# A hybrid RWKV-7 and Gated DeltaNet block: the bonus behind the pair products, dense products in groups of four, two output tiles interleaved

## The chip, the cores and the metric

The kernel runs on one core of one Trainium2 chip. The metric is the device time of one execution in microseconds; the times of the kernel before are the median, the lowest and the highest of three runs.

## What is computed

One layer of a streaming encoder over 512 positions of width 1024, all in float32. Cut to what matters here:

```python
u = rms_norm(x, norm1_g)
p = u @ w_in                                   # rwkv part, qkv, z, a, b, two gates
y_a = rwkv7_mix(...) @ rwkv_proj               # 8 heads of 64
y_b = gated_deltanet_mix(...) @ gdn_proj       # 4 heads of 128
mixed = sigmoid(gate_a) * y_a + sigmoid(gate_b) * y_b
x = x + mixed @ w_out
h = causal_depthwise_conv(rms_norm(x, norm2_g) @ ffn_up, ffn_conv_w)
h_gate, h_up = split(h)
x = x + (silu(h_gate) * h_up) @ ffn_down
return rms_norm(x, final_g)

# inside rwkv7_mix, behind the scan over positions:
y = group_norm_heads(y, ln_w, ln_b)
y = y + sum(r_h * k_h * r_k, axis=-1) * v_h    # the bonus
```

## The kernel before, in words

**Layout.** Activations lie transposed, 128 channels on the partitions and 512 positions in the free dimension, so a width of 1024 is eight K-tiles. Every dense product is made of float32 weights and activations that are each split into a high and a low half: `halves_of` (L156, L158) makes the halves `hi` (on ACT) and `lo` (on POOL or DVE in turn) of 512 columns of a weight tile `raw`, and `split` (L201 to L205) those of an activation, `uh` and `ul`.

**Dense products.** `mm3` (L173 to L185) adds lo x uh, hi x uh and hi x ul in one PSUM bank: for each half of a weight tile (four K-tiles) eight matmuls of L180 and L181 in turn, then four of L183, so 12 a half and 24 a tile. They number 2496 in mm3: 1056 for w_in, 192 for the two branch projections, 192 for w_out and 1056 for ffn_up. Banks come from three groups, D (2 banks, dense tiles), A (3) and B (3, the second stream).

**Stages by time.** First tiles to 50 us; the mixing from 50 to 430 us, in which the dense tiles of w_in run between the work of the heads; the projections of the two branches (`project(0)`, `project(1)`), 430 to 476 us; w_out, 476 to 520; ffn_up to 765; ffn_down to the end.

**The mixing.** The string `ORDER` lists its parts: R0 to R3 prepare one RWKV head pair each (`rwkv_prep`), I0 and I1, or i0 and i1, invert triangular matrices (L563 to L569 on DVE, L591 and L598 on PE), z0 to z3 hold the output gates of the DeltaNet heads, g0 to g13 dense tiles of the two merge gates, c0 and c1 are the chains over chunks of the RWKV heads (L661 to L674: matmuls of 64 rows and columns, `Z` and `SUV` evacuated between them by DVE and ACT), G0 to G3 and C0, C1 the same for the DeltaNet heads (C1's last matmul is L928). What an engine executes next is settled by a list scheduler from the program order and the priorities (`tc.high_priority`, `stream2`), not by the text alone.

**One preparation** (`rwkv_prep`) makes, on DVE, the scaled keys (L508, L510, L513, tile `BK`, one buffer for each half of the chunks), then the bonus: r * r_k * K on DVE (L515), a matmul with a block of ones on PE (L517), the product with v on DVE into `yf` (L518). Behind it, for each half h, the pairwise products of four chunks on PE into two banks (`pe`, L527, and `po`, L528) and transposes into a third (`pt`, L530), the masked copies on DVE (L534, four) and a copy on ACT (L537); at the end one scaling on DVE (L538). All these banks are of group A.

**The output projection** (`merge`, L966 to L980) takes the eight tiles of w_out one after the other. Its operand `uh`, `ul` comes from project(1): per tile DVE adds (L946, L948), ACT makes uh (L204) and DVE ul (L205).

Of the kernel before, what the change touches and what calls it, by code (L numbers as in the profile page):

```python
# [13 lines left out]
ALU = mybir.AluOpType  # L14
# [3 lines left out]
D = 1024  # L18
# [6 lines left out]
BANKS = {"D": 2, "A": 3, "B": 3}  # L25
ORDER = "R0 g0 R1 g1 g2 g3 a i0 G0 G1 z1 c0 z0 g4 g5 R2 I0 R3 C0 g6 i1 c1 g7 g8 G2 G3 g9 z3 g10 z2 g11 I1 g12 C1 g13"
RAWG = 1
UN = (range(0), range(2), range(2, 8))
NWARM = 13
OUTG = ((0, 2), (2, 4), (4, 6), (6, 8))  # L30
# [64 lines left out]
class Body:  # L95
# [74 lines left out]
        return parts  # L170


    def mm3(self, ps, parts, act, first=True, last=True):  # L173
        nc = self.nc
        k0 = 0
        for i, (wh, wl, n) in enumerate(parts):
            w = [slice(k * 128, k * 128 + 128) for k in range(n)]
            x = [act(k0 + k) for k in range(n)]
            for k in range(n):
                nc.tensor.matmul(ps, wl[:, w[k]], x[k][0], start=(first and i == 0 and k == 0), stop=False)  # L180
                nc.tensor.matmul(ps, wh[:, w[k]], x[k][0], start=False, stop=False)  # L181
            for k in range(n):
                nc.tensor.matmul(ps, wh[:, w[k]], x[k][1], start=False,  # L183
                                 stop=(last and i == len(parts) - 1 and k == n - 1))
            k0 += n  # L185

    def dense_in(self, m, act=None, tag="D", parts=None):
# [257 lines left out]
    def rwkv_prep(self, hp, first=None):  # L445
        nc = self.nc
        Rt, K, r = first or (self.rp.tile([128, 9, T], F32, tag="R", name=self.nm("R")), self.t("P"), self.t("P"))
# [4 lines left out]
        v = Rt[:, 8, :]  # L452
        if first is None:
# [5 lines left out]
        ps = self.bank()  # L459
# [8 lines left out]
                                     op0=ALU.mult, op1=ALU.add)  # L468
# [10 lines left out]
        ps = self.bank()  # L479
# [11 lines left out]
        for tl, s in ((ase, slice(0, 64)), (aso, slice(64, 128))):  # L491
            nc.vector.scalar_tensor_tensor(out=tl[s, :, 0, :], in0=kv[s], scalar=self.nkk[s, hp:hp + 1], in1=ep[s, :, 0:64],
                                           op0=ALU.mult, op1=ALU.mult)
            self.on("e").tensor_tensor(out=tl[s, :, 1, :], in0=rv[s], in1=ep[s, :, 1:65], op=ALU.mult)

        ps = self.bank()
# [8 lines left out]
        q = lambda x, s, h: x[s, h * 256:h * 256 + 256].rearrange("p (c t) -> p c t", c=4)  # L505
# [6 lines left out]
            for s, sk in ((slice(0, 64), 1), (slice(64, 128), 0)):  # L512
                self.on("c").tensor_tensor(out=bkh[h][s, :, sk, :], in0=q(K, s, h), in1=q(em, s, h), op=ALU.mult)  # L513

        nc.vector.scalar_tensor_tensor(out=r, in0=r, scalar=self.vec("r_k", hp), in1=K, op0=ALU.mult, op1=ALU.mult)  # L515
        ps = self.bank()
        nc.tensor.matmul(ps, self.con("bones"), r, start=True, stop=True)  # L517
        nc.vector.tensor_tensor(out=self.yf[:, hp, :], in0=ps, in1=v, op=ALU.mult)  # L518

        rwm = self.con("rwm")  # L520
        for h in range(2):
            pe, po, pt = self.bank(), self.bank(), self.bank()
# [8 lines left out]
            w = slice(4 * h, 4 * h + 4)  # L531
            lo, hi = slice(0, 64), slice(64, 128)
            for ps, s, tl in ((pe, lo, ntb), (pe, hi, ase), (po, hi, ntb), (po, lo, aso)):
# [3 lines left out]
            nc.scalar.activation(bkt[:, w, :], pt.rearrange("p (c t) -> p c t", c=4), AF.Copy)  # L537
        self.on("o").tensor_tensor(out=ntb[:, :, 0, :], in0=ntb[:, :, 0, :],  # L538
                                in1=rs2.unsqueeze(2).broadcast_to([128, 8, 64]), op=ALU.mult)
        return dict(ase=ase, aso=aso, ntb=ntb, bkt=bkt, v=v)  # L540

    def inv(self, x):
# [409 lines left out]
    def merge(self):  # L952
# [12 lines left out]
        self.u2p = self.pool("u2p", bufs=1, reuse_waits="tile")  # L965
        self.u2h = self.u2p.tile([128, KD, T], F32R, name="u2h")  # L966
        self.u2l = self.u2p.tile([128, KD, T], F32R, name="u2l")
        for m in range(KD):
            parts = self.unit(self.a["w_out"][m])
            ps = self.bank("D")  # L970
            self.mm3(ps, parts, lambda k: (mh[:, k, :], ml[:, k, :]))
            x = x1[:, m, :]
            g = self.vec("norm2", m)
            with tc.high_priority():
                nc.vector.tensor_tensor(out=x, in0=ps, in1=x, op=ALU.add)
                nc.scalar.activation(self.u2h[:, m, :], x, AF.Copy, scale=g)
                nc.vector.scalar_tensor_tensor(out=self.u2l[:, m, :], in0=x, scalar=g, in1=self.u2h[:, m, :].bitcast(F32),
                                               op0=ALU.mult, op1=ALU.subtract)
            self.sumsq(self.acc2, x, m == 0)
# [267 lines left out]
```

## Time and profile before

| | |
|---|---|
| time, median of 3 runs | 893.6 us (893.51 to 896.17) |
| the profiled execution: time | 897.17 us |
| the profiled execution: span from first to last instruction | 895.0 us |
| mean granted clock of TensorE | 0.992 |
| PE busy | 860.9 us, 96% |
| PE weight loads (beside the matmuls) | 677.9 us, 76% |
| DVE, ACT, POOL busy | 646.0, 473.2, 209.7 us |
| bytes moved | 84.25 MB, 94 GB/s |

PE is TensorE's matmuls, DVE is VectorE, ACT ScalarE, POOL GpSimd. The span is what the rows further down divide; the execution's own time has 2.2 us around it. A row of a timeline has the start, the duration, the engine, the line of the kernel, the tile written and the tiles read, and in brackets how long the engine sat idle before it and what ended that. Matmuls overlap: the pace is the distance of their starts, not their duration.

### The profile page before, as it was taken

Reading aid. Unit: us, or ns where it says so; the run is one execution under the profiler, and the core shown is the slowest. Engines: PE = TensorE matmul, PEld = TensorE weight load, DVE = VectorE, ACT = ScalarE, POOL = GpSimd, SP = SyncE. Lnnn points to the kernel's source line nnn. Section 1 sums busy time; section 2 is a strip of 40 time slices with the busy share of each in tenths; the row PEclk is TensorE's granted clock in tenths of the full one; section 3 lists DMA queues with packets and bytes.
Section 4 is the critical chain, followed back from the end, with each engine's and each line's share of the span. In section 5 each row is a group of like instructions: output and inputs, shape, how many; then the busy total and the mean of one; then the engine's idle time right before and its main releaser. Section 6 shows DMA issues by size and latency. Waiting matters only on the chain.

```text
span 895.0 us, 13509 instructions
## 1 busy us (share of the span) xinstructions
PE 860.9 (96%) x5046; PEld 677.9 (76%) x5046; DVE 646.0 (72%) x1247; ACT 473.2 (53%) x909; POOL 209.7 (23%) x189
## 2 busy tenths in 40 slices
PE   7989999999999999999999999999999999999996
PEld 4867677666767777667787878888888888898895
DVE  6898797874888986855476448988866666573565
ACT  7745457667443777673543455455444444444433
POOL 2231123111121221111212222222222222352431
PEclk9999999999999999999999999999999999999998
DMA  7321222121212221125352323323333332332333
GB/s 263 112 91 59 71 71 72 48 73 48 72 59 71 71 72 37 60 89 206 94 174 85 94 95 94 95 94 95 94 100 101 101 100 90 99 102 86 110 86 133
DMA packets 29746, 84.25 MB, mean 94 GB/s; under 512 B 3312, under 2 KB 5488, under 8 KB 29680
## 3 DMA queue, kind: packets, MB, share of 16 engines
q1 hardware_dynamic: 29680, 83.39, 29.3%
q8 instruction: 40, 0.66, 0.3%
q14 instruction: 26, 0.21, 0.1%
HBM read 77.61 MB, written 5.77 MB: 93 GB/s over the span
## 4 chain that ended last, share of the span: by engine, by line
PE 70%; DVE 19%; ACT 4%; issue 4%; DMA 1%; POOL 1%; SPq 0%; DVEq 0%; POOLq 0%; ACTq 0%
PE D L183 15%; PE D L180 15%; PE D L181 15%; PE D L1077 5%; PE A L1077 4%; PE B L1077 3%; DVE lo L158 2%; DVE R L534 1%; DVE P L769 1%; DMA raw<-w_in 1%; DVE invN L563 1%; DVE BK L513 1%; DVE invY L565 1%; DVE BK L508 1%; DVE R L948 1%
## 5 line engine op out<-in xcount | busy, mean ns | idle before, releaser
L158 POOL TENSOR_TENSOR lo<-raw,hi 128x512 fp32r<-128x512 f32 x124 | 170.3, 1373 | 614.4 <-ACT hi L156 590.6
L156 ACT ACTIVATE hi<-raw 128x512 fp32r<-128x512 f32 x248 | 152.9, 620 | 195.7 <-PE D L183 95.2
L180 PE MATMUL D<-uh,lo 128*128 128x512 f32 x384 | 158.3, 413 | 3.5 <-ACT uh L204 1.9
L181 PE MATMUL D<-uh,hi 128*128 128x512 f32 x384 | 157.6, 410 | 0.0
L180 PE MATMUL D<-u2h,lo 128*128 128x512 f32 x352 | 137.9, 392 | 0.0
L181 PE MATMUL D<-u2h,hi 128*128 128x512 f32 x352 | 137.8, 392 | 0.0
L183 PE MATMUL D<-ul,hi 128*128 128x512 f32 x384 | 117.8, 411 | 0.4 <-DVE ul L202 0.4
L158 DVE TENSOR_TENSOR lo<-raw,hi 128x512 fp32r<-128x512 f32 x124 | 87.7, 707 | 34.9 <-ACT hi L156 34.5
L183 PE MATMUL D<-u2l,hi 128*128 128x512 f32 x352 | 95.1, 392 | 0.0
L180 PEld LDWEIGHTS D<-uh,lo 128*128 128x128 f32 x384 | 72.7, 189 | 21.8 <-ACT uh L204 2.4
L181 PEld LDWEIGHTS D<-uh,hi 128*128 128x128 f32 x384 | 72.6, 189 | 16.0 <-issue 1.0
L994 DVE SCALAR_TENSOR_TENSOR P<-T,vecs,P 128x511 f32<-128x511 f32 x88 | 78.3, 890 | 8.4 <-ACT P L992 4.1
L183 PEld LDWEIGHTS D<-ul,hi 128*128 128x128 f32 x384 | 70.4, 189 | 17.1 <-issue 1.2
L181 PEld LDWEIGHTS D<-u2h,hi 128*128 128x128 f32 x352 | 66.1, 188 | 14.9 <-issue 0.2
L180 PEld LDWEIGHTS D<-u2h,lo 128*128 128x128 f32 x352 | 66.1, 188 | 14.7 <-issue 0.2
L183 PEld LDWEIGHTS D<-u2l,hi 128*128 128x128 f32 x352 | 66.1, 188 | 14.1
L991 DVE TENSOR_TENSOR T<-D,acc 128x512 f32<-128x512 f32 x44 | 30.3, 688 | 34.5 <-PE D L183 30.6
L992 ACT ACTIVATE P<-T,vecs 128x512 f32<-128x512 f32 x44 | 31.7, 721 | 12.1 <-DVE T L991 10.0
L563 DVE TENSOR_TENSOR invN<-invA,invY 128x60 f32<-128x60 f32 (+24 forms) x124 | 33.2, 268 | 2.6
L565 DVE TENSOR_TENSOR invY<-invY,invN 128x60 f32<-128x60 f32 (+24 forms) x124 | 33.0, 266 | 2.9
L769 DVE SCALAR_TENSOR_TENSOR P<-D,vecs,P 128x511 f32<-128x511 f32 (+2 forms) x36 | 26.6, 740 | 1.5 <-ACT P L767 1.5
L1183 ACT ACTIVATE P<-P 128x512 f32<-128x512 f32 x22 | 13.7, 624 | 18.7 <-DVE P L994 18.7
(437 smaller groups left out, 1566.1 us busy)
## 6 DMA issues: line engine op xcount, KB each, us to landing
raw<-w_in SPq DMA_DIRECT2D x44, 512.0 KB, 3.5
raw<-ffn_up SPq DMA_DIRECT2D x44, 512.0 KB, 3.6
raw<-ffn_down SPq DMA_DIRECT2D x9, 512.0 KB, 3.5
raw<-w_out SPq DMA_DIRECT2D x8, 512.0 KB, 3.6
raw<-ffn_down SPq DMA_DIRECT2D x16, 256.0 KB, 2.9
spill<-T SPq DMA_DIRECT2D x14, 256.0 KB, 2.0
R<-spill SPq DMA_DIRECT2D x14, 256.0 KB, 5.9
raw<-ffn_down SPq DMA_DIRECT2D x9, 384.0 KB, 3.1
```

Source lines behind the costliest of these rows:

```text
L156: nc.scalar.activation(hi[:, 0:w], raw[:, o:o + w], AF.Copy)
L158: self.on(str(self.halves % 4)).tensor_tensor(out=lo[:, 0:w], in0=raw[:, o:o + w], in1=hi[:, 0:w].bitcast(F32), op=ALU.subtract)
L180: nc.tensor.matmul(ps, wl[:, w[k]], x[k][0], start=(first and i == 0 and k == 0), stop=False)
L181: nc.tensor.matmul(ps, wh[:, w[k]], x[k][0], start=False, stop=False)
L183: nc.tensor.matmul(ps, wh[:, w[k]], x[k][1], start=False, stop=(last and i == len(parts) - 1 and k == n - 1))
L563: nc.vector.tensor_tensor(out=w, in0=rows[:, t, 0:t].unsqueeze(2).broadcast_to([128, t, n]), in1=Ym[:, t, c:G].unsqueeze(1).broadcast_to([ ...
L565: nc.vector.tensor_tensor(out=Ym[:, 0:t, c:G], in0=Ym[:, 0:t, c:G], in1=w, op=ALU.add)
L769: nc.vector.scalar_tensor_tensor(out=cv[:, sh:], in0=ps[:, 0:T - sh], scalar=w(3 - sh), in1=cv[:, sh:], op0=ALU.mult, op1=ALU.add)
L991: nc.vector.tensor_tensor(out=h, in0=ps, in1=self.acc2, op=ALU.mult)
L992: nc.scalar.activation(cv, h, AF.Copy, scale=w(2))
L994: nc.vector.scalar_tensor_tensor(out=cv[:, sh:], in0=h[:, 0:T - sh], scalar=w(2 - sh), in1=cv[:, sh:], op0=ALU.mult, op1=ALU.add)
L1077: nc.tensor.matmul(out, w, x, start=bank not in started, stop=stop)
```

## The change

`rwkv_prep` issues the bonus (multiply, matmul, product with v) at its end, behind both halves of the pairwise products. `mm3` gives every matmul but the first of each four a high priority, so that the scheduler keeps the four together; the order of the 12 matmuls is as before. `merge` takes w_out's tiles 0 and 1 half by half: tile 0 with K-tiles 0 to 3, tile 1 with 0 to 3, tile 0 with 4 to 7, tile 1 with 4 to 7. From line 28 on the lines move by 2 and more: L180, L181 and L183 become L185, the bonus L538, L540 and L541, the products L524, L525 and L527, the masked copies L531, the chain steps L663 and on.

```diff
--- before.py
+++ after.py
@@ -25,6 +25,8 @@
 BANKS = {"D": 2, "A": 3, "B": 3}
 ORDER = "R0 g0 R1 g1 g2 g3 a i0 G0 G1 z1 c0 z0 g4 g5 R2 I0 R3 C0 g6 i1 c1 g7 g8 G2 G3 g9 z3 g10 z2 g11 I1 g12 C1 g13"
 RAWG = 1
+
+BLK = 4
 UN = (range(0), range(2), range(2, 8))
 NWARM = 13
 OUTG = ((0, 2), (2, 4), (4, 6), (6, 8))
@@ -170,18 +172,18 @@
         return parts
 
 
+
     def mm3(self, ps, parts, act, first=True, last=True):
         nc = self.nc
         k0 = 0
         for i, (wh, wl, n) in enumerate(parts):
             w = [slice(k * 128, k * 128 + 128) for k in range(n)]
             x = [act(k0 + k) for k in range(n)]
-            for k in range(n):
-                nc.tensor.matmul(ps, wl[:, w[k]], x[k][0], start=(first and i == 0 and k == 0), stop=False)
-                nc.tensor.matmul(ps, wh[:, w[k]], x[k][0], start=False, stop=False)
-            for k in range(n):
-                nc.tensor.matmul(ps, wh[:, w[k]], x[k][1], start=False,
-                                 stop=(last and i == len(parts) - 1 and k == n - 1))
+            seq = [(t, 0, k) for k in range(n) for t in (wl, wh)] + [(wh, 1, k) for k in range(n)]
+            for q, (t, p, k) in enumerate(seq):
+                with self.tc.high_priority(offset=100000) if q % BLK else nullcontext():
+                    nc.tensor.matmul(ps, t[:, w[k]], x[k][p], start=(first and i == 0 and q == 0),
+                                     stop=(last and i == len(parts) - 1 and q == len(seq) - 1))
             k0 += n
 
     def dense_in(self, m, act=None, tag="D", parts=None):
@@ -512,11 +514,6 @@
             for s, sk in ((slice(0, 64), 1), (slice(64, 128), 0)):
                 self.on("c").tensor_tensor(out=bkh[h][s, :, sk, :], in0=q(K, s, h), in1=q(em, s, h), op=ALU.mult)
 
-        nc.vector.scalar_tensor_tensor(out=r, in0=r, scalar=self.vec("r_k", hp), in1=K, op0=ALU.mult, op1=ALU.mult)
-        ps = self.bank()
-        nc.tensor.matmul(ps, self.con("bones"), r, start=True, stop=True)
-        nc.vector.tensor_tensor(out=self.yf[:, hp, :], in0=ps, in1=v, op=ALU.mult)
-
         rwm = self.con("rwm")
         for h in range(2):
             pe, po, pt = self.bank(), self.bank(), self.bank()
@@ -537,6 +534,11 @@
             nc.scalar.activation(bkt[:, w, :], pt.rearrange("p (c t) -> p c t", c=4), AF.Copy)
         self.on("o").tensor_tensor(out=ntb[:, :, 0, :], in0=ntb[:, :, 0, :],
                                 in1=rs2.unsqueeze(2).broadcast_to([128, 8, 64]), op=ALU.mult)
+
+        nc.vector.scalar_tensor_tensor(out=r, in0=r, scalar=self.vec("r_k", hp), in1=K, op0=ALU.mult, op1=ALU.mult)
+        ps = self.bank()
+        nc.tensor.matmul(ps, self.con("bones"), r, start=True, stop=True)
+        nc.vector.tensor_tensor(out=self.yf[:, hp, :], in0=ps, in1=v, op=ALU.mult)
         return dict(ase=ase, aso=aso, ntb=ntb, bkt=bkt, v=v)
 
     def inv(self, x):
@@ -965,10 +967,20 @@
         self.u2p = self.pool("u2p", bufs=1, reuse_waits="tile")
         self.u2h = self.u2p.tile([128, KD, T], F32R, name="u2h")
         self.u2l = self.u2p.tile([128, KD, T], F32R, name="u2l")
+
+
+        mixed = lambda k: (mh[:, k, :], ml[:, k, :])
+        two = [(self.unit(self.a["w_out"][m]), self.bank("D")) for m in range(2)]
+        for q in range(2):
+            for parts, ps in two:
+                self.mm3(ps, parts[q:q + 1], lambda k: mixed(4 * q + k), first=q == 0, last=q == 1)
         for m in range(KD):
-            parts = self.unit(self.a["w_out"][m])
-            ps = self.bank("D")
-            self.mm3(ps, parts, lambda k: (mh[:, k, :], ml[:, k, :]))
+            if m < 2:
+                ps = two[m][1]
+            else:
+                parts = self.unit(self.a["w_out"][m])
+                ps = self.bank("D")
+                self.mm3(ps, parts, mixed)
             x = x1[:, m, :]
             g = self.vec("norm2", m)
             with tc.high_priority():
```

Where the scheduler puts the matmuls is seen from the order of PE's instructions. The first place is the preparation of the first head pair; `P_287` is r * r_k * K, `BK_511` and `BK_512` the two halves' keys, D tiles are dense products. Before:

```order
L183 MATMUL D_654<-ul,hi_650 128x512 x4
L517 MATMUL A_523<-P_287,cons 128x512
L527 MATMUL A_526<-R_285,BK_511 128x128
L528 MATMUL A_527<-R_285,BK_511 128x128
...
L530 MATMUL A_528<-cons,BK_511 128x128 x4
...
L527 MATMUL A_546<-R_285,BK_512 128x128
L528 MATMUL A_547<-R_285,BK_512 128x128
...
L530 MATMUL A_548<-cons,BK_512 128x128 x4
```

With the change:

```order
L524 MATMUL A_522<-R_285,BK_511 128x128
L525 MATMUL A_523<-R_285,BK_511 128x128
...
L527 MATMUL A_524<-cons,BK_511 128x128 x4
L185 MATMUL D_654<-ul,hi_650 128x512 x4
L524 MATMUL A_542<-R_285,BK_512 128x128 x3
L525 MATMUL A_543<-R_285,BK_512 128x128 x3
...
L527 MATMUL A_544<-cons,BK_512 128x128 x4
L185 MATMUL D_785<-ul,hi_777 128x512 x4
L540 MATMUL A_564<-P_287,cons 128x512
```

The bonus matmul stood ahead of both halves' products and now stands behind them; the second half's products come behind four dense matmuls instead of seven.

The second place is the third step of the second RWKV chain, c1 (`B_2974` its bank). Before:

```order
L180 MATMUL D_3768<-uh,lo_3761 128x512
L181 MATMUL D_3768<-uh,hi_3760 128x512
L661 MATMUL B_2974<-SUV_2961,R_2016 64x64
L180 MATMUL D_3768<-uh,lo_3761 128x512
L662 MATMUL B_2974<-SUV_2962,R_2016 64x64
L181 MATMUL D_3768<-uh,hi_3760 128x512
L661 MATMUL B_2974<-SUV_2961,R_2387 64x64
L662 MATMUL B_2974<-SUV_2962,R_2387 64x64
L180 MATMUL D_3768<-uh,lo_3761 128x512
```

With the change:

```order
L185 MATMUL D_3729<-uh,hi_3725 128x512
L663 MATMUL B_2974<-SUV_2961,R_2016 64x64
L664 MATMUL B_2974<-SUV_2962,R_2016 64x64
L663 MATMUL B_2974<-SUV_2961,R_2387 64x64
L664 MATMUL B_2974<-SUV_2962,R_2387 64x64
L185 MATMUL D_3729<-ul,hi_3725 128x512 x4
L669 MATMUL B_2974<-Z_2979,R_2016 64x64 x2
```

The eight matmuls of the step (each row here is two) were cut by single dense ones and now stand together; over the whole program the runs that hold such matmuls go from 83 to 68, and the runs of dense matmuls from 149 to 135.

The third place is the begin of w_out on PE; `D_4720` is its tile 0, `D_4759` before and `D_4731` in the change its tile 1. Before:

```order
L183 MATMUL D_4720<-ul,hi_4712 128x512 x4
L180 MATMUL D_4720<-uh,lo_4717 128x512
...
L183 MATMUL D_4720<-ul,hi_4716 128x512 x4
L180 MATMUL D_4759<-uh,lo_4752 128x512
...
L183 MATMUL D_4759<-ul,hi_4751 128x512 x4
```

With the change:

```order
L185 MATMUL D_4720<-ul,hi_4712 128x512 x4
L185 MATMUL D_4731<-uh,lo_4724 128x512
...
L185 MATMUL D_4731<-ul,hi_4723 128x512 x4
L185 MATMUL D_4720<-uh,lo_4717 128x512
...
L185 MATMUL D_4720<-ul,hi_4716 128x512 x4
```

Tile 0's second half now stands 12 matmuls later.

## Rows read from the trace of the kernel before

**Rows 1.** The page, busy time by engine, and the clock in 40 slices.

```profile
PE 860.9 (96%) x5046; PEld 677.9 (76%) x5046; DVE 646.0 (72%) x1247; ACT 473.2 (53%) x909; POOL 209.7 (23%) x189
...
PEclk9999999999999999999999999999999999999998
```

**Rows 2.** Waits of PE: engine, bank, line, releaser: us, times, longest.

```profile
PE A L517 <- DVE P L515: 5.2, 4, 2.0
PE D L180 <- ACT uh L204: 1.9, 1, 1.9
...
PE B L598 <- ACT invY L594: 0.8, 1, 0.8
```

**Rows 3.** Windows: length, busy time (and instructions) by engine, granted clock, DMA.

```profile
69.00:72.50 3.50, 3.50 (x22) 2.88 (x21) 3.49 (x7) 0.51 (x1) 0.00 (x0) 0.51 0.27 70
...
80.00:120.00 40.00, 36.68 (x188) 27.26 (x187) 33.59 (x80) 20.91 (x46) 5.42 (x6) 1.00 0.20 73
...
482.00:485.50 3.50, 3.50 (x9) 2.72 (x10) 1.31 (x2) 1.05 (x2) 1.27 (x1) 0.52 0.41 140
485.50:489.00 3.50, 3.50 (x17) 2.80 (x16) 1.46 (x3) 1.89 (x4) 0.22 (x1) 1.00 0.45 121
```

**Rows 4.** Timeline of PE at the begin of w_out: start us, duration us.

```profile
475.67 0.40 PE L180 MATMUL D<-uh,lo 128*128 128x512 f32 x1
...
478.47 0.39 PE L180 MATMUL D<-uh,lo 128*128 128x512 f32 x1
...
481.96 0.69 PE L180 MATMUL D<-uh,lo 128*128 128x512 f32 x1 [1.94 <-ACT uh L204]
```

**Rows 5.** Timelines of ACT and of POOL in the same stretch.

```profile
478.09 0.63 ACT L204 ACTIVATE uh<-R 128x512 fp32r<-128x512 f32 x1 [1.96 <-DVE R L948]
...
481.28 0.63 ACT L204 ACTIVATE uh<-R 128x512 fp32r<-128x512 f32 x1 [2.04 <-DVE R L948]
...
476.21 1.30 POOL L158 TENSOR_TENSOR lo<-raw,hi 128x512 fp32r<-128x512 f32 x1 [5.00 <-ACT hi L156]
```

**Rows 6.** Timeline of PE, a chain step cut in three.

```profile
348.49 0.39 PE L181 MATMUL D<-uh,hi 128*128 128x512 f32 x1
...
349.49 0.33 PE L662 MATMUL B<-SUV,R 128*64 128x64 f32 x2
...
350.78 0.39 PE L181 MATMUL D<-uh,hi 128*128 128x512 f32 x1
```

**Rows 7.** Timeline of PE, a chain step in one run.

```profile
368.47 0.39 PE L181 MATMUL D<-uh,hi 128*128 128x512 f32 x1
368.79 0.27 PE L661 MATMUL B<-SUV,R 128*64 128x64 f32 x1
...
369.50 0.39 PE L181 MATMUL D<-uh,hi 128*128 128x512 f32 x1
```

**Rows 8.** Timeline of PE, the bonus of the first and second head pair.

```profile
67.75 1.12 PE L517 MATMUL A<-P,cons 128*128 128x512 f32 x2 [1.85 <-DVE P L515]
...
94.27 1.13 PE L517 MATMUL A<-P,cons 128*128 128x512 f32 x2 [2.00 <-DVE P L515]
```

**Rows 9.** Timeline of DVE in the first two preparations.

```profile
66.94 0.75 DVE L515 SCALAR_TENSOR_TENSOR P<-P,vecs,P 128x512 f32<-128x512 f32 x1
68.45 0.75 DVE L373 SCALAR_TENSOR_TENSOR P<-D,vecs,P 128x511 f32<-128x511 f32 x1 [0.76 <-ACT P L372]
...
70.97 2.69 DVE L534 TENSOR_TENSOR R<-A,cons 64x512 f32<-64x512 f32 x4
...
95.43 0.69 DVE L518 TENSOR_TENSOR yf<-A,R 128x512 f32<-128x512 f32 x1 [1.22 <-PE A L517]
```

**Rows 10.** Timelines of DVE and PE at the first inverse.

```profile
148.99 0.70 DVE L569 STREAM_TRANSPOSE invA<-invN 128x512 f32<-128x512 f32 x1
...
138.86 0.39 PE L180 MATMUL D<-uh,lo 128*128 128x512 f32 x1
...
149.75 1.20 PE L591 MATMUL B<-invA,R 32*32 32x32 f32 x64 [0.21 <-DVE invA L569]
```

## The prediction

> **What bounds the kernel.** I read the page's busy times first: PE is busy 860.9 us of a span of 895.0, DVE 646.0 [rows 1]. So the kernel is a stream of matmuls, and a change can win in three ways only: less idle time of PE, a higher granted clock, or fewer nanoseconds per matmul. The idle time is 895.0 - 860.9 = 34 us, the kernel's start and end included; in the view of PE's waits the largest cause is the bonus matmul of a head pair (5.2 us in 4 waits), and the next is the operand uh of the output projection (1.9 us, once) [rows 2]. The clock row of the page is 9 in every slice but the last [rows 1], yet a table of narrow windows finds two stretches at about half, 69.0 to 72.5 us and 482.0 to 485.5 us, and full clock right behind [rows 3]; each begins right behind one of those waits. What a half-clock stretch costs I read from its own row: 9 matmuls start in 482.0:485.5 and 17 in the next 3.5 us [rows 3], so some 6 to 8 dense matmuls of 0.23 us are lost, 1.5 us. The dense pace is 12 matmuls in 478.47 - 475.67 = 2.80 us, 0.233 us each [rows 4].
>
> **1. Output projection, two tiles interleaved.** Tile 0 starts its second half at 478.47 and at 481.96 has stood 1.94 us idle for the operand uh number 7 [rows 4], which ACT starts at 481.28 and takes 0.63 us for [rows 5]. In the change the 12 matmuls of tile 1's first half stand there: 12 x 0.233 = 2.8 us, until 481.27; uh number 7 is then wanted 6 matmuls later, at 482.7, 0.8 us after it is there. Tile 1's weights are in time: the low half that POOL makes starts at 476.21 and takes 1.30 us [rows 5], done 0.96 us before 478.47. The interleave puts nothing ahead of uh number 7 on ACT or DVE; that chain runs at one operand per 3.19 us (481.28 - 478.09 [rows 5]), slower than PE's 12 x 0.233 = 2.8 per tile, so it lags PE whenever PE arrives, and a gain upstream shifts both. Saved: 1.94 us of wait and the 1.5 us of half clock behind it, **-3.4 us**. Bounds: 0, if uh number 7 is late again by 2 us, to -3.4.
>
> **2. Dense products in groups of four.** A dense matmul stays full price wherever it stands; what the change saves is the price of a switch between dense matmuls and the 64-row matmuls of the recurrent chains. At 348.49 a chain step of eight such matmuls is cut in three by single dense ones: from 348.49 to 350.78, 2.29 us, four dense matmuls start (4 x 0.233 = 0.93), so the step costs 1.36 us [rows 6]. At 368.47 the same eight stand together: 1.03 us with two dense (0.47), so 0.56 us [rows 7]. Two more runs cost 0.80 us, 0.40 per run. By the order, the runs that hold such small matmuls fall from 83 to 68; seven of the fifteen are of exactly this chain step, the others of shorter kinds. 7 x 0.40 = 2.8 us and 15 x 0.40 = 6.0 us are the bounds; I take eleven, **-4.4 us**.
>
> Against this speaks a rule of the Trainium skill ("TensorE: Matmul & The Clock Gate", "What happens when you issue a matmul"): the queue of TensorE pulls the next weight load ahead of running matmuls when row groups do not conflict or the load goes to the background buffer, so that a neighbour of another shape need not cost anything. By it this part would be 0. The two rows above do not agree, 1.36 us against 0.56; it stays as a rival.
>
> **3. The bonus behind the pair products.** Today the bonus matmul waits for the multiply of DVE at 66.94 and PE sits idle 1.85 us and, in the second pair, 2.00 us [rows 8]; with the small waits of pairs 2 and 3 that is 5.2 us [rows 2], and one fall of the clock (1.5). All 6.7 us go. What is late next: PE now meets the pair products first, whose inputs DVE writes just ahead of the same multiply, and only three A banks exist. DVE's order is hardly changed: the multiply (0.75 us) still stands ahead of the mask multiplies of the first half (four in 2.69 us) [rows 9], and these empty the banks that the second half's products need. I walked the first pair by these durations: first half waits about 1.1 us for its inputs, second half about 1.0 for a bank, the bonus 0.5; second pair 1.2, 1.4, 0.4; the last two pairs, 0.3 and 0.8. That is again 6.7 us. What remains is that DVE loses waits of its own: 1.22 us before the bonus multiply of the second pair and 0.76 at 68.45 [rows 9]; it leaves the second pair some 2.7 us earlier. I book **-1.0 us**. Bounds: -6.7 (no new wait) to +10.1: if in all four pairs the second half waits for the whole 2.69 us and the clock falls (1.5), 16.8 - 6.7. The value lies with my walk since DVE works through these 2.69 us while PE has a group of four and four transposes to do.
>
> **4. What the new order moves elsewhere.** The order places the first matmuls of the triangular inverse behind dense number 360 instead of 400. PE passes number 360 at 138.86 today; the input comes from DVE at 148.99 + 0.70 = 149.7, and the wait at 149.75 is only 0.21 [rows 10]. DVE has some 8 instructions fewer ahead of it (five convolution steps, one low half and two more, 0.6 to 0.75 each: 5.9 us) and starts 2.7 us earlier, so it is done at 141.1. PE would wait 141.1 - 138.9 = 2.2 us, and longer by what it gained upstream, about 3 us. In exchange the waits now at 145 to 153 us go, 0.8 at the next inverse step [rows 2], 0.2 and 0.5 beside it: 1.5 us. Net **+1.5 us**; bounds -1.5 (DVE is there) to +6 (the 2.7 us don't come, and the clock falls). The second DeltaNet chain ends 33 to 44 dense matmuls later (some 8 to 10 us), with 72 dense matmuls (16.8 us) still ahead of its consumer and about 11 us of finishing work: cover 5.8 us, cost 0; if that cover is gone, the second projection waits. Loads, bytes and the feed-forward part (pure dense work) are untouched.
>
> **Sum:** -3.4 - 4.4 - 1.0 + 1.5 = -7.3 us. The profiled execution took 897.2 us, 3.6 above the median of 893.6; the forecast is 889.9 for it and **886.3 us** for the median.
>
> **Rivals.**
> A. *Switches cost nothing saved* (the rule above; or the switches saved are the cheap ones, such as groups of 128-row matmuls): part 2 is 0 and the sum -2.9, 890.7 us. For: half of the fifteen runs aren't of the priced kind. Against: rows 6 and 7. Chance 0.15.
> B. *The waits really vanish*: DVE's lead spreads, preparations cost 3 us less and the inverse is fed in time (-1.5): -3.4 - 4.4 - 4.0 - 1.5 = -13.3, 880.3 us. For: DVE has no wait left in the preparations. Against: DVE is busy nearly without a break there, each step 0.6 to 0.75 us behind the last [rows 9]. Chance 0.17.
> C. *Slower, by the A banks*: the products of each second half stand in PE's queue ahead of whole groups of dense matmuls, so PE can't fill the wait. With 2.69 us and a fall of the clock in every pair, -3.4 - 4.4 + 10.1 + 1.5 = +3.8, 897.4 us. It decides once the new idle time in the preparations passes 6.7 + 6.3 = 13 us, 3.2 us per pair where I have 1.7. For: only three banks; a wait of 1.85 us was enough for a fall at 69 us. Against: 2.00 us at 94.27 brought none, the clock of 80 to 120 us is 1.00 [rows 3]. Chance 0.10.
> D. *About no change*: half of C's waits, -2 to +2 us, 893 us. Chance 0.10. That the change doesn't do what it says is no case: in the order the groups and the interleave stand.
>
> **The numbers.** The forecast (-4.5 to -10.5 us) has 0.48. Measurements of this kernel tell 0.3%, 2.7 us, from no change. Faster by more: forecast 0.48, B 0.17, two thirds of A 0.10, and 0.02 of D: 0.77. Slower by more: most of C and a little of D, 0.09. The rest, 0.14, is within. The range 878.5 to 892.0 holds the forecast, A, two thirds of B and a third of D, 0.8 together; below it lies the rest of B, above it C.
>
> **What would show it.** Right: no wait at the output projection and full clock at 480 us; PE's waits view without the bonus line but with the pair products and the bonus matmul (released by DVE mask multiplies or ACT copies) at about 6 to 7 us in sum; chain steps of eight small matmuls in one run at 0.56 us; a wait of 2 to 4 us at the inverse near 138 us. Wrong: dense matmuls beside the chains as far apart as before (A); more than 13 us of waits in the preparations, or more than two half-clock stretches (C); the inverse without a wait (B).

## The result, and the profile after

The change takes the kernel from 894.2 to 889.7 us (medians of 4 runs each): ratio 0.995, 95% interval 0.9937 to 0.9962, 4.5 us faster. Timed again beside three variants it gave 889.2 us against 894.6, ratio 0.9944 (0.9927 to 0.9960). The forecast was 886.3 us, a gain of 7.3, with a range of 878.5 to 892.0: the sign and the range held, the gain was some 60% of the sum.

The profiled execution of the changed kernel took 889.34 us, 0.4 below its median; its span is 887.6. That of before took 897.17, 3.0 us above its median, so two profiles laid side by side show 7.8 us where the medians show 4.5. The first experiment shows where most of that comes from. The page of the change (busy time; granted clock in 40 slices):

```profile
PE 854.3 (96%) x5046; PEld 679.3 (77%) x5046; DVE 653.5 (74%) x1247; ACT 466.0 (53%) x905; POOL 210.3 (24%) x189
...
PEclk9999999999999999999999999999999999999998
```

PE is busy 6.6 us less than in [rows 1] with the same number of instructions, and still the engine that is never long idle. The largest waits of PE in the change (engine, bank, line, releaser: us, times, longest):

```profile
PE A L794 <- DVE G L775: 2.9, 2, 1.8
PE B L675 <- ACT SUV L672: 2.2, 6, 0.8
PE A L524 <- DVE BK L515: 1.5, 2, 1.3
PE D L303 <- ACT hi L158: 1.5, 1, 1.5
PE B L593 <- DVE invA L571: 1.4, 1, 1.4
PE D L185 <- DVE R L375: 1.4, 1, 1.4
```

Both large waits of [rows 2] are gone, and nothing of 5 us stands in their place; the waits are now many and short, at the DeltaNet preparation (L794), the chains (L675), the pair products (L524), the second inverse (L593). The windows that answer to [rows 3] (length, PE, PEld, DVE, ACT, POOL busy, granted clock, DMA):

```profile
69.00:72.50 3.50, 3.29 (x22) 2.48 (x21) 3.45 (x6) 1.60 (x3) 0.00 (x0) 1.00 0.00 0
478.00:481.50 3.50, 3.50 (x16) 2.81 (x15) 2.66 (x3) 2.10 (x5) 1.48 (x2) 1.00 0.49 147
480.00:520.00 40.00, 40.00 (x174) 32.18 (x173) 21.52 (x31) 19.08 (x31) 9.14 (x8) 1.00 0.30 96
```

Neither half-clock stretch (a granted clock of 0.5) is there in this execution. That is not so in every execution: of the ten timed runs of the change (four here, six further down) five have a mean granted clock of 0.997, like this one, and take 888.4 to 889.3 us; the other five have 0.994 or 0.995 and take 889.8 to 890.8, on the mean 1.4 us more.

For all kernels below I split the time from the first dense matmul of mm3 to the first of w_out into two accounts, summed from the timeline of PE: **waits** (what stands in brackets) and **matmul time** (from each start to the next, less the wait). Beside them stand the time at half clock in that stretch, and the sum of both accounts at the pair products and the bonus matmul of the four preparations.

| kernel | start to w_out | waits | matmul time | at half clock | pair products and bonus | ratio to before |
|---|---|---|---|---|---|---|
| before | 453.6 | 18.8 | 434.7 | 3.4 | 19.1 | 1 |
| e1 interleave alone | 451.9 | 17.1 | 434.8 | 3.4 | 16.4 | 0.9967 |
| e2 groups of four alone | 452.9 | 24.3 | 428.7 | 6.8 | 18.1 | 0.9996 |
| e3 bonus alone | 454.4 | 16.4 | 438.0 | 3.4 | 19.2 | 1.0019 |
| e4 interleave and groups | 451.4 | 24.2 | 427.1 | 3.4 | 16.6 | 0.9956 |
| the change | 450.3 | 20.2 | 430.0 | 0 | 18.0 | 0.9950 |
| e9 the change again | 450.1 | 20.2 | 429.9 | 0 | 18.0 | 0.9944 |

One trace is one execution, and two of them differ also where the program does not. Ahead of w_out, before and e1 issue the same instructions, and so do e2 and e4. Their traces differ by 1.5 to 1.7 us up to w_out and by up to 2.7 us in the column of the pair products, so differences of that size between two rows say nothing by themselves.

The rest of the gain lies in w_out: from its first dense matmul to the 48th behind it 14.95 us before and 11.18 in the change.

### The profile page after: what moved, and what is told of

Same layout as the page of the kernel before. It is cut to its first block, busy times and chain, and to the rows that moved or that the text cites. A ratio compares the mean times of both kernels' runs of the same rounds, so it can differ in the third digit from the quotient of the medians.

```text
span 887.6 us, 13504 instructions
## 1 busy us (share of the span) xinstructions
PE 854.3 (96%) x5046; PEld 679.3 (77%) x5046; DVE 653.5 (74%) x1247; ACT 466.0 (53%) x905; POOL 210.3 (24%) x189
## 4 chain that ended last, share of the span: by engine, by line
PE 68%; DVE 16%; ACT 6%; issue 3%; POOL 0%; DVEq 0%; ACTq 0%; POOLq 0%
PE D L185 43%; PE D L1089 5%; PE A L1089 4%; PE B L1089 3%; PE B L185 2%; DVE invN L565 2%; PE A L185 2%; DVE invY L567 2%; DVE P L771 1%; DVE lo L160 1%; DVE R L531 1%; DVE BK L510 1%; DVE BK L515 1%; ACT hi L158 1%; PE B L663 1%
## 5 line engine op out<-in xcount | busy, mean ns | idle before, releaser
L185 PE MATMUL D<-uh,lo 128*128 128x512 f32 x384 | 160.5, 418 | 2.7 <-DVE R L375 1.4
L185 PE MATMUL D<-uh,hi 128*128 128x512 f32 x384 | 151.4, 395 | 0.0
L185 PE MATMUL D<-u2h,lo 128*128 128x512 f32 x352 | 137.9, 392 | 0.0
L185 PE MATMUL D<-u2h,hi 128*128 128x512 f32 x352 | 137.8, 392 | 0.0
L185 PE MATMUL D<-ul,hi 128*128 128x512 f32 x384 | 109.1, 406 | 0.0
L185 PE MATMUL D<-u2l,hi 128*128 128x512 f32 x352 | 95.1, 392 | 0.0
L185 PEld LDWEIGHTS D<-uh,lo 128*128 128x128 f32 x384 | 72.2, 188 | 21.3 <-issue 3.1
L1006 DVE SCALAR_TENSOR_TENSOR P<-T,vecs,P 128x511 f32<-128x511 f32 x88 | 81.8, 929 | 6.9 <-ACT P L1004 2.6
L185 PEld LDWEIGHTS D<-uh,hi 128*128 128x128 f32 x384 | 72.3, 188 | 14.6 <-issue 1.0
L185 PEld LDWEIGHTS D<-ul,hi 128*128 128x128 f32 x384 | 69.3, 188 | 16.3 <-issue 1.0
L185 PEld LDWEIGHTS D<-u2h,hi 128*128 128x128 f32 x352 | 66.1, 188 | 14.9 <-issue 0.2
L185 PEld LDWEIGHTS D<-u2h,lo 128*128 128x128 f32 x352 | 66.1, 188 | 14.7 <-issue 0.2
L185 PEld LDWEIGHTS D<-u2l,hi 128*128 128x128 f32 x352 | 66.1, 188 | 14.1
L565 DVE TENSOR_TENSOR invN<-invA,invY 128x60 f32<-128x60 f32 (+24 forms) x124 | 39.6, 319 | 3.0
L1004 ACT ACTIVATE P<-T,vecs 128x512 f32<-128x512 f32 x44 | 31.7, 721 | 16.5 <-DVE T L1003 14.5
L567 DVE TENSOR_TENSOR invY<-invY,invN 128x60 f32<-128x60 f32 (+24 forms) x124 | 32.3, 260 | 3.0
L1195 ACT ACTIVATE P<-P 128x512 f32<-128x512 f32 x22 | 13.7, 624 | 21.0 <-DVE P L1006 21.0
```

The lines of the kernel that those rows point to most:

```text
L185: nc.tensor.matmul(ps, t[:, w[k]], x[k][p], start=(first and i == 0 and q == 0), stop=(last and i == len(parts) - 1 and q == len(seq) - 1))
L565: nc.vector.tensor_tensor(out=w, in0=rows[:, t, 0:t].unsqueeze(2).broadcast_to([128, t, n]), in1=Ym[:, t, c:G].unsqueeze(1).broadcast_to([ ...
L567: nc.vector.tensor_tensor(out=Ym[:, 0:t, c:G], in0=Ym[:, 0:t, c:G], in1=w, op=ALU.add)
L1004: nc.scalar.activation(cv, h, AF.Copy, scale=w(2))
L1006: nc.vector.scalar_tensor_tensor(out=cv[:, sh:], in0=h[:, 0:T - sh], scalar=w(2 - sh), in1=cv[:, sh:], op0=ALU.mult, op1=ALU.add)
L1195: nc.scalar.activation(g, g, AF.Silu)
```

## Experiments

The medians of before beside the three sets of runs were 894.6 (e1 to e4), 893.9 (e5 to e8) and 894.6 us (e9 to e12). Theory: each part acts where the profile shows it, and what the groups save in switches comes back as waits. The rivals stand in each expectation. The edits are shown against the changed kernel; "bonus ahead" puts the four bonus lines back in front of `rwm = self.con("rwm")`.

**e1, the interleave alone** (bonus ahead, no groups).

```diff
-BLK = 4
+BLK = 1
```

> The kernel before with the interleave of the first two output tiles alone. Theory (the three parts act where the profile shows them and hardly touch each other): the wait of 1.94 us at the output projection goes, and the half-clock stretch behind it in those executions that have one (1.4 us): 2 to 3.5 us less than before, the stages ahead of it unchanged to 0.3 us. Rival (the place where PE arrives early only moves the wait to tile 1): 0 to 1 us less, with a wait of 1 us or more within the next 24 dense matmuls.

891.1 us against 894.6: ratio 0.9967 (0.9954 to 0.9979), 3.0 us. From the first dense matmul of w_out on, its trace is 3.7 us shorter than that of before, and there is no wait there. The theory holds in that. (The trace shows more than the medians. In before's profiled execution, with a mean granted clock of 0.992, a half-clock stretch followed the wait; before's other runs go from 0.990 to 0.997, and not all of them need have had it.) Whether the stages ahead are unchanged to 0.3 us can't be told from two traces. Ahead of w_out this is the same program as before, and yet it gets there 2.0 us earlier in its trace, with this line for the bonus:

```profile
PE A L519 <- DVE P L517: 3.2, 3, 1.9
```

Before had 5.2 us in 4 waits [rows 2]. The half-clock stretch lay at 83.4 us here and at 69.1 there (length, busy time by engine, granted clock, DMA):

```profile
83.40:86.80 3.40, 3.40 (x9) 2.62 (x8) 3.32 (x6) 2.48 (x4) 1.38 (x2) 0.50 0.33 130
```

At 69.1 us it slows the pair products of the first head pair, and DVE waits 1.26 us for them, where it waits 0.17 us in e1. The keys of the second pair take DVE 2.76 us there and 1.71 in e1. So DVE's multiply for the second bonus ends at 94.22 us in before and at 92.19 in e1, and PE waits 2.0 us for it in before and not at all in e1. So the stretch moves from execution to execution, and waits come and go with it; 2 us of a difference between two profiles are here no effect of an edit.

**e2, the groups of four alone** (bonus ahead, w_out tile by tile as before).

```diff
-        two = [(self.unit(self.a["w_out"][m]), self.bank("D")) for m in range(2)]
...
+            parts = self.unit(self.a["w_out"][m])
+            ps = self.bank("D")
+            self.mm3(ps, parts, lambda k: (mh[:, k, :], ml[:, k, :]))
```

> The kernel before with the groups of four alone. Theory: what the fewer switches save (some 3.5 us) is given back as waits of PE for the chains, the inverses and the DeltaNet preparations, which grew by some 3.5 us outside the RWKV preparations between the two profiles: -1 to +1 us. Rival (those waits came with the moved bonus, which lets DVE run ahead and the inverse be placed earlier): 3 to 4.5 us less, with the waits outside the preparations as before.

894.5 us against 894.6: ratio 0.9996 (0.9985 to 1.0007). The switches are saved and the end does not move. The windows over the mixing say it in one row each, first of e1, then of e2:

```profile
100.00:430.00 330.00, 318.09 (x2467) 233.47 (x2467) 249.94 (x674) 206.17 (x467) 56.76 (x65) 1.00 0.24 75
```

```profile
100.00:430.00 330.00, 311.33 (x2468) 233.71 (x2467) 251.21 (x671) 199.61 (x457) 56.33 (x65) 1.00 0.25 76
```

In the same 330 us PE issues the same number of matmuls, 2467 and 2468, and is busy 6.8 us less: it stands idle instead. Where, says the view of PE's waits of e2:

```profile
PE B L675 <- ACT SUV L672: 3.0, 7, 0.8
...
PE B L593 <- DVE invA L571: 1.8, 2, 0.9
...
PE A L823 <- ACT T L817: 1.7, 2, 1.0
PE B L905 <- DVE G L903: 1.6, 2, 0.9
PE D L185 <- DVE invY L567: 1.4, 1, 1.4
PE D L185 <- DVE R L375: 1.4, 1, 1.4
```

Of these e1 has 1.5 at L675, 1.0 at L593, 1.0 at L823, 0.7 at L905 and neither wait of a dense matmul (L185); these two ended, by the view's account, when DVE ended a step of an inverse (L567) and of a token shift (L375). The theory holds, the rival (waits as before, 3 us or more gained) falls.

**e3, the bonus alone** (no groups, w_out as before).

```diff
-BLK = 4
+BLK = 1
```

> The kernel before with the bonus behind the pair products alone. Theory: the waits in the four preparations fall by some 2.5 us, and the half-clock stretch at 69 us (1.3 us) goes: 2.5 to 4 us less. Rival (the groups of four make the room for it; without them the second half's products come sooner and wait longer for banks): -1 to +1 us, with 6 us or more of waits at the pair products and the bonus matmul.

895.9 us: ratio 1.0019 (1.0010 to 1.0029), slower by 1.7 us. Neither expectation came: it is not faster, as the theory had it, and the rival's 6 us or more of waits at the pair products and the bonus are 3.8, its range of -1 to +1 us is passed. Against before the waits fell (16.4 us in all for 18.8) and the matmul time rose by more (438.0 for 434.7). Pair products and bonus take 19.2 us, where the two traces of the order with the bonus ahead have 19.1 (before) and 16.4 (e1); the half-clock stretch of e3 and of before lies on the first preparation, that of e1 between two. Clear of that are the pair products alone, without the bonus: 13.5 us of matmul time in e3, 9.7 and 9.0 in the other two. How time can go without a wait is seen in the changed kernel, the second half's products of the first preparation on PE, and the masked copies of the first half on DVE:

```profile
69.50 0.93 PE L524 MATMUL A<-R,BK 64*128 64x128 f32 x6
70.50 0.60 PE L525 MATMUL A<-R,BK 64*128 64x128 f32 x3
...
71.59 0.50 PE L185 MATMUL D<-uh,lo 128*128 128x512 f32 x1
```

```profile
67.48 0.75 DVE L538 SCALAR_TENSOR_TENSOR P<-P,vecs,P 128x512 f32<-128x512 f32 x1
68.27 0.68 DVE L531 TENSOR_TENSOR R<-A,cons 64x512 f32<-64x512 f32 x1
68.99 0.75 DVE L375 SCALAR_TENSOR_TENSOR P<-D,vecs,P 128x511 f32<-128x511 f32 x1
69.75 0.69 DVE L531 TENSOR_TENSOR R<-A,cons 64x512 f32<-64x512 f32 x1
```

The kinds L524 and L525 take 64 of the array's 128 rows each, from different halves of the partitions; where they are issued in turn, as in the rows of before below, two of them start within 0.01 us of each other. Here six rows of L524 (three matmuls, put together by the scheduler as in the order above) run alone for a microsecond. The first L525 starts at 70.50, just behind the masked copy that ends at 69.75 + 0.69 = 70.44; the semaphore that it waits for is set at 70.46. The half takes 2.09 us, from 69.50 to 71.59; the second half of the same preparation before:

```profile
73.73 0.37 PE L527 MATMUL A<-R,BK 64*128 64x128 f32 x1
73.73 0.37 PE L528 MATMUL A<-R,BK 64*128 64x128 f32 x1
...
74.82 0.66 PE L530 MATMUL A<-cons,BK 128*128 128x128 f32 x4
```

1.09 us, from 73.73 to 74.82. One microsecond is lost to the bank and to the order that allows for it, and no bracket shows it (in the second preparation a part of it does, 0.5 us at L525, released by L531). Ahead of that copy on DVE stand the bonus multiply (L538) and a step of the token shift (L375).

**e4, interleave and groups** (bonus ahead).

```diff
+        nc.vector.scalar_tensor_tensor(out=r, in0=r, scalar=self.vec("r_k", hp), in1=K, op0=ALU.mult, op1=ALU.mult)
+        ps = self.bank()
+        nc.tensor.matmul(ps, self.con("bones"), r, start=True, stop=True)
+        nc.vector.tensor_tensor(out=self.yf[:, hp, :], in0=ps, in1=v, op=ALU.mult)
+
         rwm = self.con("rwm")
```

> The changed kernel with the bonus back ahead of the pair products (interleave and groups of four kept). Theory: as the interleave alone, 2 to 3.5 us less than before. Rival (groups of four are the gain): 5 us or more less than before, no slower than the full change.

890.3 us: ratio 0.9956 (0.9944 to 0.9969). That is 3.9 us by the ratio (2.8 to 5.0), a little more than the theory's 2 to 3.5: 3 us for the interleave and about one for the groups on top of it, at the edge of what can be told. The rival's 5 us are not reached.

**e5, e6, e7, groups of two, six and twelve**, each as e4.

```diff
-BLK = 4
+BLK = 2
```

> Interleave kept, bonus ahead as before, groups of two instead of four. Theory (grouping saves switches and gives it back as waits, both in step with the size of the group): against the interleave alone the matmul time up to the output projection falls by 2 to 3 us (5.4 with four), PE's waits grow by 1.5 to 3.5 us (6.4 with four); in sum within 1 us of it, 3 to 4 us less than before. Rival (the waits come from the new order as such, not from the size): waits grow by 5 us or more, and the time is 1 to 3 us above the interleave alone.

> Interleave kept, bonus ahead as before, groups of six. Theory: matmul time 6 to 8 us less, PE's waits 7 to 10 us more than with the interleave alone: 0 to 2 us slower than it. Rival (waits do not follow the size): waits as with four, matmul time lower, so 1 to 2 us faster than groups of four.

> Interleave kept, bonus ahead as before, groups of twelve. Theory: matmul time some 9 us less and PE's waits 12 us or more above the interleave alone, since a chain step now comes only every 2.8 us of dense work and the chains end late: 3 us or more slower than it, at or above the time before. Rival (waits do not follow the size): faster than groups of four by 2 us or more.

| kernel (interleave, bonus ahead) | us | ratio (interval) | waits | matmul time | at half clock | matmul time less 0.43 a us at half clock |
|---|---|---|---|---|---|---|
| e1 no groups | 891.1 | 0.9967 (0.9954 to 0.9979) | 17.1 | 434.8 | 3.4 | 433.3 |
| e5 two | 900.9 | 1.0069 (1.0044 to 1.0093) | 21.6 | 436.2 | 17.1 | 428.9 |
| e4 four | 890.3 | 0.9956 (0.9944 to 0.9969) | 24.2 | 427.1 | 3.4 | 425.6 |
| e6 six | 906.0 | 1.0136 (1.0118 to 1.0155) | 31.6 | 436.2 | 30.7 | 423.0 |
| e7 twelve | 929.2 | 1.0402 (1.0382 to 1.0422) | 44.9 | 445.6 | 64.9 | 417.7 |

The waits grow with the size, as the theory has it, though by more than it gave: over e1 4.5 us for two (1.5 to 3.5 expected), 14.5 for six (7 to 10), 27.8 for twelve (12 or more). The matmul time falls with the size once the half clock is taken out (last column, an estimate: the price of 0.43 us is from e12, below). But the times do not follow: twos should have come within 1 us of e1 and are 10 us slower, sixes 15, where 0 to 2 were expected, and twelves 38. For two and six both theory and rival fail. I had left out a third account, the clock. It is not only in the traces: over all its runs the mean granted clock is 0.995 in e1, 0.994 in e4, 0.983 in e5 and e6 and 0.962 in e7. Twos have two more stretches than e1 in their trace, each twice as long (and that execution took 896.9 us, 4 us less than their median); one of them (length, PE, PEld, DVE, ACT, POOL busy, granted clock):

```profile
226.30:233.00 6.70, 6.70 (x30) 5.25 (x30) 3.65 (x10) 3.33 (x7) 0.00 (x0) 0.50 0.00 0
```

It begins behind a wait of 1.9 us at 225.6, among inverse steps and preparation products. Fours have little more of it than e1 (3.4 us in e4's trace, 6.8 in that of e2, which is the same program ahead of w_out), which no part of my reasoning foresees; why the order of two, six and twelve brings more is open. In the large groups the cover of the last DeltaNet chain is gone too, and the second projection waits for its operand, in e6 and in e7:

```profile
PE B L185 <- ACT yh L206: 5.1, 1, 5.1
```

```profile
PE B L185 <- ACT yh L206: 6.1, 1, 6.1
```

**e8, the bonus multiply on POOL** (the full change otherwise).

```diff
-        nc.vector.scalar_tensor_tensor(out=r, in0=r, scalar=self.vec("r_k", hp), in1=K, op0=ALU.mult, op1=ALU.mult)
+        nc.gpsimd.tensor_tensor(out=r, in0=r, in1=K, op=ALU.mult)
+        nc.gpsimd.tensor_tensor(out=r, in0=r, in1=self.vec("r_k", hp).broadcast_to([128, T]), op=ALU.mult)
```

> The full change, with the bonus multiply taken from DVE: POOL does it in two products (r by K, then by r_k), so that DVE goes from the scaled keys straight to the masked copies. Theory (the multiply on DVE, kept ahead of the masked copies, holds the banks of the second half's products): PE's time at the pair products and the bonus, waits included, falls from 18.0 us by 2 to 4, and the kernel is 1.5 to 3 us faster than the full change. Rival (what the preparations gain is lost at the next wait for DVE, in the chains and the inverses): the preparations gain, yet the time is within 1 us of the full change.

899.8 us: ratio 1.0061 (1.0047 to 1.0075). Neither expectation: the preparations lose, 22.7 us at pair products and bonus for 18.0. One reason shows on DVE. The four scaled-key products of DVE take twice as long beside POOL, in e8 and in the change:

```profile
65.88 3.46 DVE L515 TENSOR_TENSOR BK<-P,T 64x256 f32<-64x256 f32 x4
```

```profile
65.70 1.77 DVE L515 TENSOR_TENSOR BK<-P,T 64x256 f32<-64x256 f32 x4
```

POOL's two products run in e8 from 65.93 to 68.61 us, just beside these. DVE is rid of 0.75 us and pays 1.7, so the experiment does not say what the multiply's place is worth. Nor is that all of the loss: e8's trace has 10.2 us at half clock beside the first two preparations (69.2 to 76.0 and 93.1 to 96.5 us), where that of the change has none. By the price below that is some 4 of the 10 us by which it comes later to w_out, an estimate.

**e9 to e12, the change again and three other places of the bonus.** e10 takes the bonus' bank from group B, e11 puts the bonus between the halves (`if h == 0:` at the end of the loop), e12 puts it ahead in the program, in a bank of B.

```diff
-        ps = self.bank()
+        ps = self.bank_of("B")
         nc.tensor.matmul(ps, self.con("bones"), r, start=True, stop=True)
```

> The changed kernel itself, timed again beside the three variants below. Theory (on top of the groups the moved bonus is worth about nothing: what it takes from the waits ahead of the bonus comes back in the second half's products): the ratio to before lies within 0.2% of the kernel that keeps the bonus ahead (0.9956). Rival (on top of the groups it pays): ratio 0.993 or lower.

> The full change, with the bonus matmul in a bank of group B instead of A. Theory (the second half's products wait for the banks of the first half, which DVE empties; the bonus' own bank plays no part): PE's time at the pair products and the bonus, waits included, stays at 17 to 19 us (18.0), the kernel within 1.5 us of the full change. Rival (the bonus takes one of three A banks and so holds the next tile up): that time falls to 15 us or less and the kernel is 2 us faster.

> The full change, with the bonus between the two halves' products instead of behind them. Theory: the bonus matmul finds its input ready (no wait, as in the full change) but takes the bank that the second half's first product wants, whose two kinds of products then no longer run side by side: pair products and bonus 17 to 20 us, kernel within 1.5 us of the full change. Rival (with the bonus between, DVE has the time to empty the banks): 15 us or less, 2 us faster.

> Interleave and groups of four, the bonus in the program ahead of the pair products as before, but in a bank of group B, which leaves the order on PE to the scheduler: it sets the bonus matmul among the first half's products. Theory: the bonus wait (3.65 us with groups and the bonus ahead) goes and the three A banks serve the halves alone: pair products and bonus 14 to 17 us (16.6 with the bonus ahead in A), kernel 0 to 2 us faster than the full change, the best of all. Rival (B banks are wanted by the chains, whose steps then wait): waits in the chains grow by 2 us or more, slower than the full change.

| kernel | us | ratio (interval) | waits | matmul time | at half clock | pair products and bonus |
|---|---|---|---|---|---|---|
| e9 the change | 889.2 | 0.9944 (0.9927 to 0.9960) | 20.2 | 429.9 | 0 | 18.0 |
| e10 bonus in B | 895.9 | 1.0018 (1.0005 to 1.0031) | 22.4 | 434.0 | 6.8 | 23.2 |
| e11 bonus between | 891.7 | 0.9970 (0.9957 to 0.9982) | 21.6 | 430.3 | 0 | 20.7 |
| e12 bonus ahead, in B | 904.3 | 1.0113 (1.0077 to 1.0149) | 23.6 | 448.6 | 44.4 | 32.4 |

e9 lies within 0.2% of e4, as the theory said; whether the bonus is worth anything on top of the groups stays open between nothing and 2 us. e11 is near what the theory gave (20.7 us against 17 to 20; 2.4 us slower than e9 against 1.5). e10 and e12 are outside both theories: with the bank from B the scheduler sets the bonus matmul ahead of the second half (e10) or among the first half's products (e12), and pair products and bonus take longer, a part of that at half clock (e10's first stretch begins at 67.6 us, e12's at 67.9). In e12 the waits at the chains' matmuls did not grow (3.9 us against 4.7 in e9), so its rival falls as well; 44 us at half clock are most of the loss, by the following price. e12's six runs differ much in their clock: 899.13 us at a mean clock of 0.989, 911.49 at 0.973, which is 12.4 us for 0.016 x 895 / 0.5 = 28.6 us more at half clock, 0.43 us per us. A line through all six gives 0.41 and one through e5's seven runs 0.39; the runs of the other kernels differ too little to tell. So a stretch of 3.4 us costs 1.3 to 1.5 us, an estimate with which the 1.4 us between the two kinds of runs of the change agree. No variant beat the change.

## Why the prediction was right and wrong

**What bounds the kernel:** right. In the change PE is never idle for long, and the effects that the traces show are waits, switches, the clock and, which I had not named, products that no longer run side by side.

**Part 1, the interleave:** right. Forecast -3.4, in the trace -3.77 (14.95 to 11.18 us), alone -3.0 by the ratio. The operand that PE waited for is there in time. The timeline of PE and of ACT in the change, in answer to [rows 4, 5]:

```profile
474.74 0.39 PE L185 MATMUL D<-uh,lo 128*128 128x512 f32 x1
...
477.54 0.39 PE L185 MATMUL D<-uh,lo 128*128 128x512 f32 x1
```

```profile
477.57 0.63 ACT L206 ACTIVATE uh<-R 128x512 fp32r<-128x512 f32 x1 [2.04 <-DVE R L950]
```

Tile 1's first half runs from 474.74 to 477.54, and uh number 7 is done at 478.20, ahead of the seventh matmul from 477.54 on, at 478.94: 0.7 us to spare, 0.8 forecast.

**Part 2, the groups:** the switches are saved, the gain was not there. I forecast 4.4 us of switches saved, 6.0 at most; e2 has 6.1 us less matmul time than before, with 3.4 us more at half clock, and e4, with as much of it as e1, has 7.7 less than e1. So the price read from [rows 6, 7], or the number of switches, was if anything too low. The eight matmuls of a chain step (L663, L664) show it: on the mean of the 16 steps 0.71 us of matmul time before and 0.59 in the change. The prediction set the Trainium skill's rule on weight loads ("TensorE: Matmul & The Clock Gate", "What happens when you issue a matmul") against this part. The prediction's reading of it, that a neighbour of another shape need cost nothing, does not hold here; the page says no more than that the next weight load is pulled ahead, and what the price of a switch consists of no run here shows. The sum of rival A, 890.7 us, is close to the measured time all the same, for another reason: the time comes back as waits.

**The step that failed is part 4**, and with it the step from a saved switch to a saved microsecond. Part 4 priced one wait that the new order brings, the first inverse, at +1.5 us and the cover of the second DeltaNet chain at 0, and had no term for the waits of the other chains, the second inverse and the DeltaNet preparations. In fact the first inverse has no wait at all in the change: DVE's last step for it ends at 136.34 + 0.71 = 137.05 us and PE is there at 137.49:

```profile
136.34 0.71 DVE L571 STREAM_TRANSPOSE invA<-invN 128x512 f32<-128x512 f32 x1
```

That is 12.6 us earlier than in [rows 10], where I had worked out 8.6. (An inverse without a wait was my sign for rival B; its time, 880.3 us, did not come.) And the waits that I had not priced came to 5.4 us in e2 (18.8 to 24.3) at the chains, the inverses, the DeltaNet preparations and two dense matmuls; in the change the waits outside the pair products and the bonus rose from 13.7 to 16.8 us. A chain step can only stand between two groups, and PE waits for whatever isn't done when its place comes.

**Part 3, the bonus:** that the move gives back what it takes was right, the way it does so only in part. I forecast 6.7 us of old price against 6.7 of new waits, and 1.0 of gain from DVE's lead. Of the new waits 3.4 us came, all at the pair products and none at the bonus. The rest is lost side-by-side running, which no list of waits shows: 12.7 us of matmul time at the pair products, where before they took 9.7 and in e4 8.9, both without a wait. In sum pair products and bonus take 18.0 us in the change, 19.1 in the trace of before and 16.4 in that of e1: even, or 1.6 us worse, within what two traces differ by. Alone the bonus costs 1.7 us. With the groups the waits fall from 24.2 (e4) to 20.2 us and the matmul time rises from 427.1 to 430.0, though e4's trace has 3.4 us at half clock and that of the change none: the 1.1 us between the two traces are no more than that stretch costs. So whether DVE's lead is worth anything, and why the bonus is harmless with the groups and costs 1.7 us without them, stays open. The parts don't add: -3.0, -0.4 and +1.7 alone (by the ratios) make -1.7, together -4.5 to -5.

**The sum** was -3.4 - 4.4 - 1.0 + 1.5 = -7.3. Against its own trace it came out: 889.9 us was forecast for an execution like the profiled one, and the profiled execution of the change took 889.34 (up to w_out -3.3 us for -3.9 forecast, behind that -3.8 for -3.4). But the forecast took the same 7.3 us off the median, and the profiled execution of before stood 3.6 us above the median on record then (3.0 above that of four runs), in part by the very waits that the sum removes: 2.0 of the 5.2 us at the bonus are not in e1's trace of the same program. By this account most of the shortfall lies there. With what the timed runs show the sum reads: interleave -3.0, groups about -1 on top of it, bonus -0.5 to -1 on top of both, the last two at the edge of what can be told.

There is luck in it. That the parts up to w_out add up in one pair of traces is luck, since the groups alone gave 0 and the bonus alone +1.7. And the range took in rival A: 889.7 us is 1.0 from A's 890.7 and 3.4 from the forecast.

**Rivals:** C's mechanism (the second half's products held up by a bank) is seen in the rows of e3 above; it did not come at C's price: the new loss at the pair products is 3.4 us of waits and 3.0 to 3.8 of matmul time in all four pairs, where C had 16.8 with the clock. That it is what makes e3 slower is likely and not shown. B did not come.

## What to carry to other kernels

On an engine that is busy nearly all the time, a saved switch is only worth something if what stands behind it is ready sooner: take the matmul time and the waits as two accounts, and look at the instructions per fixed stretch of time rather than at busy time. Know where the profiled execution stands among the timed ones before you take a sum read from it off a median: what made that execution slow may be what the sum removes. A list of waits misses what is lost when two kinds of matmuls that ran side by side come one after the other. Price a new order by every place where an engine meets another, not by the one that moved most.

## What the hardware showed unexpectedly

- The half-clock stretch of one program lay at 69.1 us in one execution and at 83.4 in another, and waits of 2 us came and went with it. The same wait of 1.85 us at the first bonus was followed by a fall of the clock in the one (the stretch at 69.1) and by none in the other. The price is some 0.4 us per us. Up to w_out groups of two, six and twelve had 17, 31 and 65 us of it in their traces, groups of four 3.4 and 6.8.
- Two products of POOL beside DVE made four DVE products take 3.46 us, where without them they take 1.77.
